# Reordering the retention stage of a hybrid trunk on Trainium2: projections of the first pair ahead of its keys, keys of the next pair ahead of the mixing of a pair

## The chip, the cores and the metric

The kernel runs on one core of one Trainium2 chip. The core has five engines that work side by side: TensorE (PE) for matmuls, VectorE (DVE) and ScalarE (ACT) for elementwise work on SBUF and PSUM, GpSimd (POOL) for elementwise work on SBUF, and SyncE (SP), which here only issues DMA transfers. Each engine takes its instructions in the order of its own queue. The metric is the time of one execution on the device, in microseconds, as the median of several runs.

## The reference, cut to what matters

A trunk of two layers works on 1024 latent tokens and 256 context tokens with 1024 channels. Each layer normalises and modulates its input, projects it once, gives the columns of that projection to three groups of heads (a pooling mixer, a 2-D neighbourhood attention, a bidirectional retention), joins their outputs, projects again, and runs a gated MLP. The retention is the part that matters here; it has six heads of 64 channels and goes over chunks of 128 tokens.

```python
def step(s, blk):
    qb, kb, vb = blk
    s_new = s * c_dec[None, :, None, None] + jnp.einsum('bhcd,bhce->bhde', kb * k_dec[None, :, :, None], vb)
    ...
    a = jnp.einsum('bhid,bhjd->bhij', qb, kb) * intra[None]
    y = jnp.einsum('bhij,bhje->bhie', a, vb) + jnp.einsum('bhid,bhde->bhie', qb, s) * q_dec[None, :, :, None]
    return s_new, y
...
def retention_output(y, gate, gn_g):
    ...
    mu = jnp.mean(y, axis=-1, keepdims=True)
    var = jnp.mean((y - mu) ** 2, axis=-1, keepdims=True)
    yn = ((y - mu) * lax.rsqrt(var + EPS)).reshape(B, L, RET_DIM) * gn_g.astype(jnp.float32)
    return (jax.nn.silu(gate.astype(jnp.float32)) * yn).astype(gate.dtype)
```

Both directions are computed and added. Query and key are rotated by a rotary embedding first (rows and columns of the token grid). The pooling mixer takes the difference between a moving mean over 2, 4, 8 or 16 tokens and the token itself, and multiplies it by a small matrix per group.

## The kernel before

Channels lie on the 128 partitions and tokens along the free axis. Tokens are cut into three parts: 512 and 512 latent tokens and 256 context tokens (`PARTS`). Every product of a projection is made of three matmuls of split operands (a high and a low half of the weights and of the input, lines 194 to 196), eight of these triples per part. The last layer needs no context output, so there queries and gates have two parts instead of three.

A projection is `feed` (line 329): it takes the next weights of a list, and for each part it takes one of two PSUM banks (tag `g`), runs 24 matmuls, and hands the bank to a body that drains it. The list is `plan` (lines 111 to 123): the weights are loaded, split and used strictly in that order, up to two ahead of their use, so it has to agree with the order of the calls. In the list, columns 9, 10, 11 of `w_in` are the queries of the three pairs of heads, 12 to 14 their keys, 15 to 17 their values, 18 to 20 their gates. Keys and values of the first two pairs, and the pooling mixer's input, are projected during the attention as its fillers and parked in DRAM (`r_dram`).

The stage is `ret()` (line 508), after the attention `nbr()` (line 337). Its pieces are:

- `tables()` (line 567): loads `dm` and makes the decay matrix `M` of each head with two Exp on ACT (lines 572 and 573) and three operations on POOL. Its scratch `e` has tag `qw`, `dm` has tag `ru`.
- `keys(p)` (line 590): for pairs 0 and 1 it loads key and value from `r_dram` into two tiles of tag `rw` (lines 595 and 596), for pair 2 it projects them (lines 601 and 605). It rotates the key (`rotary`, line 578, scratch `ru`), transposes values and keys on PE (lines 615 and 622, PSUM tag `t`), scales the keys by the decay into `kd` (lines 627 and 629), multiplies them with the values (line 634, `pk`, PSUM tags `sc` and `s`), and runs a scan over ten chunks on DVE that makes the states `S` (line 643).
- `query()` (line 646): projects the query, copies it from PSUM to `qw` (line 652) and rotates it into `qr`, which has one buffer. Its context part is copied straight to `qr` (line 582).
- `gate(p)` (line 658): projects the gate and applies Silu on ACT into `yn` (line 662, two buffers).
- `pool_mean(i)` and `pool_out(i)` (lines 526 and 554): the pooling mixer. It loads its input into `pb` (tag `rw`), makes moving sums on DVE in `sab`, which shares its one buffer with `kd`, multiplies on PE (line 559, `pps`, PSUM tag `o`), scales on ACT (line 560) and stores to `y_dram`.
- `mix(p, kr, vv, S, qr)` (line 665): in two or three blocks of up to four chunks, scores (line 677, `pa`, PSUM tag `s`), scores times `M` (line 679, `at`), query times state (line 684, `pf`, PSUM tag `sc`), scores times values (line 690, `py`, PSUM tag `o`), group normalisation on DVE, ACT and POOL (lines 692 to 703), a transpose back (line 706, `yps`, PSUM tag `t`) and the product with the gate (line 708).

PSUM tags `t` and `s` have two banks each, `sc` and `o` one each. The tile framework puts in all waits. It also orders the instructions of each engine when the program is built, by a timeline of its own: the order of the program text is a priority and the order in which buffers of one tag are handed out, but an instruction whose inputs are ready may be put ahead of earlier ones. `reuse_waits="tile"` lets a new pool start on addresses of an old one as soon as the single tiles there are done with.

After the stage, the outputs are loaded back from `y_dram` into `yna` (line 745), split, and the output projection `wo` starts (line 774); it adds into `h`, loaded at line 1541 or 1545, with the operation of line 782.

Of the kernel before, what the change touches and what calls it, by code (L numbers as in the profile page):

```python
# [45 lines left out]
def tile_trunk(ctx, tc, xT, ctxT, cc, ccT, w_mod, w_mod0, colp, w_in, pool_bd, rpbU, lgp, w_out, w_up, w_down, fing,  # L46
# [62 lines left out]
    fillers = (21, 22, 12, 15, 13, 16)  # L109
    plan, made, used, groups = [], [], [0], {}  # L110
    for l in range(DEPTH):
        for h in range(HEADS):
            plan += ([(w_in[l, h // 2], 0)] if h % 2 == 0 else []) + [(w_in[l, 3 + h], 4 if l == 0 and h == 1 else 1)]
            if h > 0:
                plan.append((w_in[l, fillers[h - 1]], 0))
        plan += [(w_in[l, i], 0) for i in fillers[5:] + (9, 18, 10, 19, 14, 17, 11, 20)]
        plan += [(w_out[l, o], 5 if o >= KT - 2 else 0) for o in range(KT)]
        names = UNITS if l == DEPTH - 1 else UNITS_C
        groups[l] = [(w_up[l, 2 * g], w_up[l, 2 * g + 1]) for g in range(NF)]
        groups[l] += [(w_down[l, 2 * g], w_down[l, 2 * g + 1]) for g in range(2 * NCH)]  # L120
        plan += [((l, g), (8, n)) for n in (FIRST if l == DEPTH - 1 else FIRST_C) for g in range(2)]
        plan += [((l, g), (8, n)) for g in range(2, NF + 2 * NCH) for n in names]
        plan += [(w_down[l, NF - 2], 3), (w_down[l, NF - 1], 0)]
# [84 lines left out]
    class Sums:  # L208
# [8 lines left out]
        def add(self, h, eng=None):  # L217
            if self.first:
                nc.scalar.activation(self.acc, h, AF.Square)
                self.first = False  # L220
                return
            sq = self.pool.tile([128, self.n], F32, tag="nt", name="sq", bufs=NT)
            nc.scalar.activation(sq, h, AF.Square)
            (eng or nc.gpsimd).tensor_tensor(self.acc, self.acc, sq, op=ALU.add)
# [96 lines left out]
    def mixing(l, X, mp):  # L321
# [7 lines left out]
        def feed(body, parts=(0, 1, 2), w=None):  # L329
            w = w or weights()  # L330
            for part in parts:
                o, n = PARTS[part]
                ps = psg.tile([128, 512], F32, tag="g", name="gps")
                gemm(ps, w, X, part)
                body(ps[:, :n], part, o, n)
# [172 lines left out]
        def ret():  # L508
# [17 lines left out]
            def pool_mean(i):  # L526
                pb = ra.tile([128, W], F32, tag="rw", name="pb", bufs=2)
                sab = ra.tile([128, 2, W], F32, tag="kd", name="sab", bufs=1)
                sa, sb = sab[:, 0], sab[:, 1]
                nc.gpsimd.memset(pb[:, 0:PADX], 0.0)  # L530
                nc.gpsimd.memset(pb[:, PADX + T:T + 3 * PADX], 0.0)
                nc.gpsimd.memset(pb[:, W - PADX:W] if not last else pb[:, T + 3 * PADX:W], 0.0)
                nc.sync.dma_start(pb[:, PADX:PADX + T], r_dram[i, :, 0:T])
                if not last:
                    nc.sync.dma_start(pb[:, T + 3 * PADX:W - PADX], r_dram[i, :, T:N])
                add = lambda o, a, b: nc.vector.tensor_tensor(o, a, b, op=ALU.add)
                if i == 0:
                    add(sa[:, 1:W], pb[:, 0:W - 1], pb[:, 1:W])
                    add(sb[high, 2:W - 1], sa[high, 1:W - 2], sa[high, 3:W])
                    srcs = ((low, sa), (high, sb))  # L540
                else:
                    add(sa[:, 1:W], pb[:, 0:W - 1], pb[:, 1:W])
                    add(sb[:, 2:W - 1], sa[:, 1:W - 2], sa[:, 3:W])
                    add(sa[:, 4:W - 3], sb[:, 2:W - 5], sb[:, 6:W - 1])
                    add(sb[high, 8:W - 7], sa[high, 4:W - 11], sa[high, 12:W - 3])
                    srcs = ((low, sa), (high, sb))
                for rows, S in srcs:
                    for (a, n) in ((PADX, T), (T + 3 * PADX, C))[:1 if last else 2]:
                        nc.vector.tensor_tensor(S[rows, a:a + 8], S[rows, a:a + 8], pcs[rows, i, 0:8], op=ALU.mult)
                        nc.vector.tensor_tensor(S[rows, a + n - 8:a + n], S[rows, a + n - 8:a + n], pcs[rows, i, 8:16], op=ALU.mult)  # L550
                        nc.vector.scalar_tensor_tensor(pb[rows, a:a + n], S[rows, a:a + n], pcs[rows, i, 16:17], pb[rows, a:a + n], op0=ALU.mult, op1=ALU.subtract)
                return pb

            def pool_out(i, pb):
                pbd = pbds[i]
                for part in yparts:
                    o, n = PARTS[part]
                    ps = psp.tile([128, 512], F32, tag="o", name="pps", bufs=1)
                    nc.tensor.matmul(ps[:, :n], pbd, pb[:, offs[part]:offs[part] + n], start=True, stop=True)
                    nc.scalar.mul(pb[:, offs[part]:offs[part] + n], ps[:, :n], cp[l][:, CP_PS + i:CP_PS + i + 1])  # L560
                nc.sync.dma_start(y_dram[3 + i, :, 0:T], pb[:, PADX:PADX + T])
                if not last:
                    nc.sync.dma_start(y_dram[3 + i, :, T:N], pb[:, T + 3 * PADX:W - PADX])
# [3 lines left out]
            def tables():  # L567
                dm = rp.tile([128, 512], F32, tag="ru", name="dm", bufs=2)
                nc.sync.dma_start(dm, dmat[:, 0:512])
                for h in range(HEADS):  # L570
                    e = ra.tile([128, 128], F32, tag="qw", name="e", bufs=2)
                    nc.scalar.activation(M[:, h], dm[:, 0:128], AF.Exp, scale=lg[:, h:h + 1])
                    nc.scalar.activation(e, dm[:, 256:384], AF.Exp, scale=lg[:, 6 + h:7 + h])
                    nc.gpsimd.tensor_tensor(M[:, h], M[:, h], dm[:, 128:256], op=ALU.mult)
                    nc.gpsimd.tensor_tensor(e, e, dm[:, 384:512], op=ALU.mult)
                    nc.gpsimd.tensor_tensor(M[:, h], M[:, h], e, op=ALU.add)

            def rotary(dst, t, part, eng=nc.gpsimd):
                o, n = PARTS[part]
                dst = dst[:, o:o + n]  # L580
                if part == 2:
                    nc.scalar.copy(dst, t)
                    return
                u = rp.tile([128, 512], F32, tag="ru", name="ru", bufs=2)
                nc.vector.stream_shuffle(u, t, [(j + 16) % 32 for j in range(32)])
                eng.tensor_tensor(dst, t, rope_sb[:, 0, o:o + n], op=ALU.mult)
                nc.vector.tensor_tensor(u, u, rope_sb[:, 1, o:o + n], op=ALU.mult)
                eng.tensor_tensor(dst, dst, u, op=ALU.add)
# [57 lines left out]
            def query():  # L646
                qr = rp.tile([128, N], F32, tag="qr", name="qr", bufs=1)

                def body(ps, part, o, n):
                    if part < 2:  # L650
                        t = ra.tile([128, 512], F32, tag="qw", name="qw", bufs=2)
                        nc.scalar.copy(t, ps)
                        ps = t
                    rotary(qr, ps, part)
                feed(body, yparts)
                return qr

            def gate(p):
                yn[p] = yp.tile([128, N], F32, tag="yn", name="yn", bufs=2)

                def body(ps, part, o, n):
                    nc.scalar.activation(yn[p][:, o:o + n], ps, AF.Silu)
                feed(body, yparts)
# [49 lines left out]
                    yt[5 + p] = yn[p]  # L713

            yn = {}
            for p in range(3):
                if p == 0:
                    tables()
                kk = keys(p)
                q = query()  # L720
                gate(p)
                if p == 0:
                    for i in range(2):
                        pool_out(i, pool_mean(i))
                mix(p, *kk, q)
            st.close()

        nbr()
        ret()
        return yt, psp  # L730

# [929 lines left out]
```

## Time and profile before

| what | value |
| --- | --- |
| median of three runs | 3078.0 us (3070.67 to 3079.22) |
| the profiled execution's own time | 3069.13 us |
| its span | 3067.3 us |
| mean granted TensorE clock over the span | 0.955 |
| DVE, ACT and POOL busy | 70%, 41% and 45% of the span |
| DVE's wait for the `rope` table ends | at 457.3 us in layer 0, 2059.9 us in layer 1 |

Times inside the profile count from the start of the span. The retention stage of layer 0 begins in the last blocks of the attention near 436 us and its last mix ends near 675 us; that of layer 1 goes from about 2042 us to 2243 us. A row of a timeline gives start, duration, engine, line, operation, output from inputs, shape and count, and in brackets the idle time ahead of it with what ended it. A row of busy time by stretch gives start and end, length, busy time with the count of instructions of each engine, the clock granted to TensorE as a share of full speed, the share of the DMA engines, and GB/s. SPq and ACTq are DMA issues of these engines; PEld are weight loads of TensorE, which run beside its matmuls.

### The profile page before, as it was taken

Reading aid. Unit: us, or ns where it says so; the run is one execution under the profiler, and the core shown is the slowest. Engines: PE = TensorE matmul, PEld = TensorE weight load, DVE = VectorE, ACT = ScalarE, POOL = GpSimd, SP = SyncE. Lnnn points to the kernel's source line nnn. Section 1 sums busy time; section 2 is a strip of 40 time slices with the busy share of each in tenths; the row PEclk is TensorE's granted clock in tenths of the full one; section 3 lists DMA queues with packets and bytes.
Section 4 is the critical chain, followed back from the end, with each engine's and each line's share of the span. In section 5 each row is a group of like instructions: output and inputs, shape, how many; then the busy total and the mean of one; then the engine's idle time right before and its main releaser. Section 6 shows DMA issues by size and latency. Waiting matters only on the chain. (4 is left out here: it accounts for less than half of the span.)

```text
span 3067.3 us, 40108 instructions
## 1 busy us (share of the span) xinstructions
PE 2791.9 (91%) x14430; PEld 2338.8 (76%) x14430; DVE 2146.8 (70%) x3468; ACT 1250.0 (41%) x2404; POOL 1366.0 (45%) x894
## 2 busy tenths in 40 slices
PE   6789989989989999998999799989997999998996
PEld 4678877878778787886888688877776788886775
DVE  7887745562878787788887755446547877778996
ACT  4345542232444443444333454542223544444332
POOL 4334343323335544554555244444242555554553
PEclk8899999989999999999999899999999999999998
DMA  6333321132133434346344112121252233335441
GB/s 217 85 113 114 95 97 66 37 138 71 51 111 128 135 126 143 126 139 204 117 128 118 50 50 61 45 102 59 76 195 87 83 103 104 103 110 206 137 138 62
DMA packets 166298, 332.02 MB, mean 108 GB/s; under 512 B 49490, under 2 KB 62674, under 8 KB 165842
## 3 DMA queue, kind: packets, MB, share of 16 engines
q1 hardware_dynamic: 165812, 328.28, 32.6%
q8 instruction: 114, 1.87, 0.3%
q10 hardware_dynamic: 288, 1.18, 0.1%
q14 instruction: 84, 0.69, 0.1%
HBM read 255.20 MB, written 74.19 MB: 107 GB/s over the span
## 5 line engine op out<-in xcount | busy, mean ns | idle before, releaser
L939 PE MATMUL ua<-ph,wu 128*128 128x512 f32 x1408 | 446.0, 398 | 14.3 <-DVE ub L1039 5.3
L165 POOL TENSOR_TENSOR wu<-urb,wu 128x512 fp32r<-128x512 f32 x160 | 250.5, 1566 | 330.7 <-ACT wu L164 325.4
L194 PE MATMUL gps<-xh,wh 128*128 128x512 f32 (+1 forms) x968 | 360.9, 373 | 17.6 <-ACT vt L269 7.0
L939 PE MATMUL ubc<-ph,wu 128*128 128x512 f32 x1056 | 335.3, 399 | 39.8 <-ACT ut L1033 28.6
L165 POOL TENSOR_TENSOR wu<-ura,wu 128x512 fp32r<-128x512 f32 x192 | 306.1, 1595 | 137.4 <-ACT wu L164 137.3
L195 PE MATMUL gps<-xh,wl 128*128 128x512 f32 (+1 forms) x968 | 356.3, 368 | 0.5 <-DVE wl L181 0.5
L196 PE MATMUL gps<-xl,wh 128*128 128x512 f32 (+1 forms) x968 | 355.7, 368 | 0.0
L426 POOL TENSOR_SCALAR P<-P,rs 128x640 f32<-128x640 f32 (+2 forms) x108 | 215.7, 2010 | 247.8 <-DVE rs L421 172.7
L939 PEld LDWEIGHTS ua<-ph,wu 128*128 128x128 f32 x1408 | 262.6, 191 | 74.1 <-ACT wu L164 6.4
L165 POOL TENSOR_TENSOR wu<-S,wu 128x512 fp32r<-128x512 f32 x128 | 181.6, 1421 | 259.9 <-ACT wu L164 257.3
L939 PE MATMUL ua<-pl,wu 128*128 128x512 f32 x704 | 279.2, 397 | 0.2 <-DVE pl L835 0.2
L939 PEld LDWEIGHTS ubc<-ph,wu 128*128 128x128 f32 x1056 | 199.3, 191 | 88.3 <-ACT ut L1033 33.4
L164 ACT CAST wu<-S 128x512 fp32r<-128x512 f32 x128 | 79.5, 621 | 402.5 <-DVE S L162 356.4
L186 POOL TENSOR_TENSOR wl<-wraw,wh 128x1024 fp32r<-128x1024 f32 x54 | 134.9, 2501 | 202.7 <-ACT wh L185 189.1
L194 PEld LDWEIGHTS gps<-xh,wh 128*128 128x128 f32 x968 | 185.5, 192 | 48.3 <-ACT vt L269 7.3
L939 PE MATMUL da<-ph,wu 128*128 128x512 f32 x640 | 203.8, 400 | 13.6 <-ACT wu L164 12.8
L939 PE MATMUL ubc<-pl,wu 128*128 128x512 f32 x528 | 208.5, 395 | 0.0
L195 PEld LDWEIGHTS gps<-xh,wl 128*128 128x128 f32 x968 | 185.6, 192 | 27.2 <-issue 1.5
L196 PEld LDWEIGHTS gps<-xl,wh 128*128 128x128 f32 x968 | 185.5, 192 | 26.3 <-issue 0.5
L164 ACT CAST wu<-ura 128x512 fp32r<-128x512 f32 x192 | 119.0, 622 | 131.5 <-DVE ura L162 61.5
L939 PE MATMUL dbc<-ph,wu 128*128 128x512 f32 x480 | 150.9, 396 | 10.1 <-DVE c L1099 10.1
L939 PEld LDWEIGHTS ua<-pl,wu 128*128 128x128 f32 x704 | 133.8, 190 | 31.7 <-DVE pl L835 1.5
(296 smaller groups left out, 6844.3 us busy)
## 6 DMA issues: line engine op xcount, KB each, us to landing
gs<-g_dram SPq DMA_DIRECT2D x148, 256.0 KB, 2.7
wm<-in_w_mod_dram SPq DMA_DIRECT2D x64, 512.0 KB, 3.9
wmp<-in_w_mod_dram SPq DMA_DIRECT2D x96, 256.0 KB, 2.7
wraw<-in_w_in_dram SPq DMA_DIRECT2D x46, 512.0 KB, 3.6
ura<-in_w_up_dram SPq DMA_DIRECT2D x44, 512.0 KB, 4.0
urb<-in_w_up_dram SPq DMA_DIRECT2D x44, 512.0 KB, 5.1
g_dram<-gt SPq DMA_DIRECT2D x60, 256.0 KB, 2.9
g_dram<-c SPq DMA_DIRECT2D x44, 256.0 KB, 2.1
```

The source lines that it names most:

```text
L164: nc.scalar.copy(w[:, 0], b[name])
L165: nc.gpsimd.tensor_tensor(w[:, 1], b[name], w[:, 0].bitcast(F32), op=ALU.subtract)
L186: nc.gpsimd.tensor_tensor(wl.rearrange(flat), raw.rearrange(flat), wh.rearrange(flat).bitcast(F32), op=ALU.subtract)
L194: nc.tensor.matmul(ps[:, :n], wh[:, k], xh, start=k == 0, stop=False)
L195: nc.tensor.matmul(ps[:, :n], wl[:, k], xh, start=False, stop=False)
L196: nc.tensor.matmul(ps[:, :n], wh[:, k], xl, start=False, stop=k == KT - 1)
L426: nc.gpsimd.tensor_scalar(Pb[r][:, :w], Pb[r][:, :w], rs[:, r:r + 1], None, op0=ALU.mult)
L939: nc.tensor.matmul(ps, lt, rt, start=start and j == 0 and q == 0, stop=j == len(x) - 1 and q == 2, skip_group_check=True)
```

## The change

The loop over the three pairs is written out in another order. Query and gate of pair 0 come first, ahead of `tables()` and `keys(0)`. `keys(1)` comes after the pooling mixer and ahead of `mix(0)`. After `mix(0)` the second query is projected, then `keys(2)` with its two projections, then the second gate, and only then `mix(1)`. The third query and gate stand between `mix(1)` and `mix(2)`. The list of weights follows: columns 14 and 17 (key and value of pair 2) now stand ahead of 19 (gate of pair 1). No piece is changed inside.

```diff
-        plan += [(w_in[l, i], 0) for i in fillers[5:] + (9, 18, 10, 19, 14, 17, 11, 20)]
+        plan += [(w_in[l, i], 0) for i in fillers[5:] + (9, 18, 10, 14, 17, 19, 11, 20)]
...
             yn = {}
-            for p in range(3):
-                if p == 0:
-                    tables()
-                kk = keys(p)
-                q = query()
-                gate(p)
-                if p == 0:
-                    for i in range(2):
-                        pool_out(i, pool_mean(i))
-                mix(p, *kk, q)
+            q = query()
+            gate(0)
+            tables()
+            kk = [keys(0)]
+            for i in range(2):
+                pool_out(i, pool_mean(i))
+            kk.append(keys(1))
+            mix(0, *kk[0], q)
+            q = query()
+            kk.append(keys(2))
+            gate(1)
+            mix(1, *kk[1], q)
+            q = query()
+            gate(2)
+            mix(2, *kk[2], q)
             st.close()
```

## The prediction

> **What bounds the kernel now.** I read the page first: TensorE carries the kernel.
>
> ```profile
> PE 2791.9 (91%) x14430; PEld 2338.8 (76%) x14430; DVE 2146.8 (70%) x3468; ACT 1250.0 (41%) x2404; POOL 1366.0 (45%) x894
> ```
>
> So a change is worth what it takes from TensorE's idle time and from its time at a low clock. The change touches only the retention stage, which runs once per layer, so the next view was busy time by stretch, for layer 0 and then layer 1. The columns are stretch, length, busy time and count for PE, PEld, DVE, ACT and POOL, granted clock, DMA share and GB/s.
>
> ```profile
> 436.50:453.00 16.50, 11.82 (x76) 9.13 (x74) 9.64 (x22) 9.00 (x26) 7.14 (x5) 1.00 0.08 14
> 453.00:469.20 16.20, 9.34 (x94) 7.25 (x94) 8.38 (x25) 8.44 (x23) 9.61 (x25) 0.58 0.58 199
> 469.20:506.00 36.80, 31.86 (x162) 26.34 (x160) 30.18 (x52) 7.90 (x13) 13.76 (x6) 0.91 0.12 43
> 506.00:622.00 116.00, 116.00 (x735) 97.79 (x735) 54.11 (x116) 27.58 (x52) 41.47 (x26) 1.00 0.14 47
> 622.00:634.50 12.50, 8.60 (x111) 6.64 (x109) 8.20 (x27) 6.96 (x14) 4.14 (x3) 1.00 0.50 177
> 634.50:652.00 17.50, 17.50 (x75) 15.53 (x76) 13.46 (x27) 10.66 (x24) 0.00 (x0) 0.53 0.42 168
> 652.00:669.00 17.00, 17.00 (x96) 13.41 (x94) 9.78 (x21) 2.77 (x6) 1.65 (x1) 0.99 0.00 0
> 669.00:678.20 9.20, 2.58 (x9) 1.30 (x8) 6.90 (x17) 2.60 (x7) 2.64 (x2) 0.71 0.71 240
> ...
> 2042.00:2054.00 12.00, 10.65 (x67) 8.72 (x67) 5.76 (x11) 6.94 (x17) 6.09 (x3) 1.00 0.16 53
> 2054.00:2072.00 18.00, 10.45 (x98) 7.87 (x97) 9.95 (x29) 9.53 (x26) 10.42 (x25) 0.63 0.48 164
> 2072.00:2090.00 18.00, 14.89 (x69) 11.37 (x68) 17.81 (x29) 3.89 (x5) 9.24 (x5) 0.97 0.03 5
> 2090.00:2102.00 12.00, 12.00 (x50) 8.64 (x52) 7.42 (x11) 1.69 (x3) 0.00 (x0) 0.74 0.37 136
> 2102.00:2190.00 88.00, 88.00 (x562) 74.03 (x559) 38.51 (x78) 21.80 (x40) 33.95 (x20) 1.00 0.14 44
> 2190.00:2211.00 21.00, 15.39 (x131) 11.76 (x130) 17.92 (x41) 6.62 (x13) 10.11 (x7) 0.92 0.34 116
> 2211.00:2240.00 29.00, 28.02 (x148) 23.88 (x148) 21.14 (x39) 10.78 (x21) 1.89 (x2) 0.82 0.37 137
> 2240.00:2250.00 10.00, 4.96 (x14) 3.85 (x15) 3.45 (x5) 1.77 (x3) 2.66 (x2) 0.66 0.74 258
> ```
>
> Three things are to be seen. The middle (506 to 622, and 2102 to 2190) is full at clock 1.00: nothing can be gained there. The entry (436.5 to 506) has 4.7 + 6.9 + 4.9 = 16.5 us idle in layer 0, and 1.35 + 7.55 + 3.1 = 12.0 us (2042 to 2102) in layer 1. The end (622 to 678.2) has 3.9 + 6.6 us idle, and 17.5 us at clock 0.53, which is 17.5 x 0.47 = 8.2 us lost. In layer 1 the end has 5.6 + 1.0 + 5.0 us idle and about 28 x 0.18 = 5 us lost to the clock. Over both layers idle time is 27.0 + 23.6 us and busy time times (1 - clock) about 16 + 15 us. So 82 us is the most that any order of this stage could save.
>
> **Why TensorE idles.** Next I read the timeline of each engine around those places.
>
> ```profile
> 436.42 0.39 PE L196 MATMUL gps<-xl,wh 128*128 128x512 f32 x1
> ...
> 468.31 1.07 ACT L652 COPY qw<-gps 128x512 f32<-128x512 f32 x2 [0.61 <-POOL M L576]
> ...
> 520.37 0.70 PE L559 MATMUL pps<-pb,pbd 128*128 128x256 f32 x2
> 526.08 1.00 PE L690 MATMUL py<-vv,at 128*128 128x64 f32 x8
> ...
> 526.90 0.69 DVE L679 TENSOR_TENSOR at<-pa,M 128x512 f32<-128x512 f32 x1 [10.43 <-PE py L690]
> ...
> 578.37 0.37 ACT L605 COPY vw<-gps 128x256 f32<-128x256 f32 x1 [2.97 <-PE gps L196]
> ...
> 621.52 0.61 PE L706 MATMUL yps<-ident,tm 128*128 128x128 f32 x4
> 621.97 0.38 PE L615 MATMUL vps<-ident,vw 128*128 128x128 f32 x2
> ```
>
> These rows show one rule: buffers of one tag are handed out in the order of the program text. The copies of the first query (`qw`) wait until 468 for `tables()` to give up `e`, which shares tag `qw`, though the second of their PSUM banks was filled with the matmul at 436.42; with both banks of tag `g` held, no projection can run, and the next one starts at 469.23 (shown below). `mix(0)`'s `py` comes only after the last `pps`, both on the single bank `o`. `keys(2)`'s transposes wait until 621.97 for the last `yps` of `mix(1)`, both on tag `t`, though `vw` was complete at 578.7. So keys and mixes alternate in a strict chain, and once the projections run out, the chain is bare.
>
> **The change, part by part.**
>
> *First query and gate ahead of tables and keys.* Nothing is added but order. I price one projection from its first and last matmul:
>
> ```profile
> 469.23 0.38 PE L194 MATMUL gps<-xh,wh 128*128 128x256 f32 x1
> ...
> 472.07 0.28 PE L196 MATMUL gps<-xl,wh 128*128 128x256 f32 x1
> 472.19 0.40 PE L194 MATMUL gps<-xh,wh 128*128 128x512 f32 x1
> ...
> 477.43 0.39 PE L196 MATMUL gps<-xl,wh 128*128 128x512 f32 x1
> ```
>
> A 512-column part is 24 matmuls in 5.5 us, a 256-column part 3.0 us, so a projection is 13.9 us in layer 0 and 10.9 us in layer 1. With `qw` first in its tag, each copy runs when its part is complete, the second at about 437; the banks come free, and the query's third part and the gate (3.0 + 13.9 = 16.9 us) can lie in the 11.5 us idle before 469. The rotation itself still waits for the rope table, whose load is issued late:
>
> ```profile
> 451.28 0.38 SPq L520 DMA_DIRECT2D rope_sb<-in_rope_dram  x1
> ```
>
> If the place of `qr` is no sooner free, the third part holds one bank until then and the gate runs on the other. Behind them come the second query and the first part of the keys' third projection, which fills a bank and then waits, since `kw` needs a slot of tag `rw` that the pool mixer gives up only through its store and reload:
>
> ```profile
> 508.49 0.32 SPq L595 DMA_DIRECT2D kw<-r_dram  x1
> ...
> 523.35 0.32 SPq L596 DMA_DIRECT2D vw<-r_dram  x1
> ```
>
> Up to 506 the old order did 16.9 us of these projections and one and a half parts more (8.2); the new one may do 16.9 + 13.9 + 5.5. That is 11.2 us ahead, less about 3 us of `mix(0)` that now waits for `keys(1)`: I take 8 us. The bounds are 0 (the idle time only moves behind 469) and 16.5 (all of it goes). In layer 1 the same count gives 7, between 0 and 12.0.
>
> What it costs: `keys(0)` gets its `ru` buffers after the query and `dm`, so I put it 3 to 5 us later; DVE's pool means (busy 30.18 of 36.8 us) then end near 501 rather than 498. It delays no TensorE work that is ready, so I count nothing; uncovered it is those 3 to 5 us per layer. The DMA of `dm` moves behind the first `ru` on SP's queue, past loads that wait for nothing later.
>
> *Silu ahead of Exp.* The first gate now runs between the attention's Exp and the tables' Exp, so ScalarE changes tables twice more per layer:
>
> ```profile
> 473.74 1.28 ACT L662 ACT_TABLE_LOAD   x1
> ```
>
> That is 4 x 1.28 = 5.1 us on an engine busy 8.4 of 16.2 us there; I count zero, up to 5 us if it lands in the attention's last chain. [...]
>
> *keys(1) ahead of mix(0), keys(2) ahead of mix(1).* Work is the same; the chain loses its bare keys. `keys(1)` now runs where `mix(0)` was blocked anyway (before 526), and `keys(2)` runs while gate and query of the third pair still fill TensorE. At the end the rows to go are these, and what is then late is the load of `h`:
>
> ```profile
> 632.12 2.38 DVE L643 SCALAR_TENSOR_TENSOR S<-S,cdec,pk 128x64 f32<-128x64 f32 x10 [0.62 <-PE pk L634]
> ...
> 634.46 1.20 PE L677 MATMUL pa<-qr,kr 64*128 64x128 f32 x8 [2.37 <-DVE S L643]
> ...
> 678.22 0.79 PE L194 MATMUL ops<-xh,wh 128*128 128x512 f32 x1 [2.31 <-DVE h L782]
> ```
>
> The wait for `h` (6.6 us idle) stays, since its buffers lie where the last mix works. Of the other 3.9 + 8.2 = 12.1 us in layer 0 I take half, 6, and give back 2 for new stalls of the in-order engines: 4 us, between -12 and +12. In layer 1, of 6.6 + 5 I take 4 and give back 3: 1 us, within the same bounds. [...]
>
> *The order of two weight loads* (14 and 17 ahead of 19) follows the calls; its cost is nothing, since the same bytes go in the same buffers. If it were not matched, projections would multiply the wrong weights, which is no matter of time.
>
> **The sum.** Layer 0: 8 + 4; layer 1: 7 + 1; together 20 us. The profiled execution took 3069.1 us (span 3067.3), so 3049 on its scale. It lies 9 us under the median of the runs shown, 3078.0, and I forecast on the median: 3058.
>
> **The rivals.**
>
> *The idle time only moves.* Both `g` banks can be stuck: in layer 0 the second query's third part goes straight to `qr`, which has one buffer and is held until `mix(0)` ends, and the other bank waits for `kw`. For it: between 486 and 506 TensorE would have little but pool outputs. Against it: 8 us of the entry's work really is earlier. Advance and new gap cancel: 3075.
>
> *Slower: mix(0) queued behind keys(1).* By the rule of tags, `pa` and `pf` (banks `s`, `sc`) now wait for `keys(1)`'s `pk`, hence for the reload of `vw`. If the pool outputs crawl as now, `vw` lands at about 526 (issue 523.35), and `keys(1)`, which before took
>
> ```profile
> 555.91 0.38 PE L615 MATMUL vps<-ident,vw 128*128 128x128 f32 x2
> ...
> 580.87 1.42 DVE L643 SCALAR_TENSOR_TENSOR S<-S,cdec,pk 128x64 f32<-128x64 f32 x7
> ```
>
> 26 us, ends at 552. Then come `mix(0)` with 35 (30 from its first `py` at 526.08 to 555.91, and my estimate of 5 for the `pa` and `pf` that were done before), `keys(2)` with 20 (between the 12.5 of its bare stretch and these 26), `mix(1)` with 39 (582.3 to 621.5) and `mix(2)` with 38 (634.46 to the row below): the mixes end at 684, against 673 now.
>
> ```profile
> 672.93 1.12 PE L706 MATMUL yps<-ident,tm 128*128 128x128 f32 x4 [3.15 <-DVE tm L703]
> ```
>
> That is +11 in layer 0; layer 1, whose pool outputs have two parts instead of three and whose reload thus comes sooner, I leave at zero: 3089. It decides from the point where `keys(1)`'s scan in layer 0 ends later than about 540. Against it: `pps` crawls now because `pa` stood ahead of it in TensorE's queue (4.9 us idle up to 506), and `pa` is now gone from there; I expect the scan to end near 526.
>
> *More than forecast.* With the scan at 526 the same count ends the mixes at 526 + 35 + 20 + 39 + 38 = 658, 15 us earlier, and the low clock at the end may go too (8.2 us). Some 20 us in each layer give 3038. Against it: the middle is full at clock 1.00 now, so the chain can shorten only as far as TensorE's own work is done earlier, and that advance was counted at 8 and 7 us.
>
> **How the numbers follow.** Forecast 0.50, idle time moves 0.20, slower 0.13, more 0.17. About 0.3% (9 us) is what a measurement of this kernel can tell from no change, so faster means under 3069. The forecast case lies there nine times in ten: faster 0.45 + 0.17 = 0.62, same 0.20 + 0.05 = 0.25, slower 0.13. The range reaches from a little beyond the strong case to the cancelled one and its spread, 3030 to 3082; it leaves out the slower case and the far ends, under 0.2.
>
> **What would show it.** Right, step by step: the first `qw` copy before 440 instead of 468; TensorE busy over 0.9 from 437 to 469; `keys(1)`'s scan before 540 and ahead of `mix(0)`'s first `py`; `vps` of `keys(2)` ahead of `mix(1)`'s `pa`; no wait for `S` ahead of `mix(2)`; two more table loads per layer. Wrong: a gap of over 10 us between 475 and 530 with both `g` banks full, mixes that end after 673, or a low clock that stays over the end of the stage although `keys(2)` is gone from it.

## The result and the profile after

The changed kernel takes 3104.3 us (median of 4 runs, 3097.64 to 3109.88), the kernel before 3074.3 us beside it (3070.63 to 3079.22). The ratio is 1.0097, with a 95% interval of 1.0081 to 1.0112: about 30 us **slower**, where 3058 us had been forecast with a range of 3030 to 3082.

First the line of busy time from the page of the changed kernel. TensorE has the same number of instructions; ScalarE has six more than the 2404 of before.

```profile
PE 2800.5 (90%) x14430; PEld 2347.6 (76%) x14430; DVE 2153.1 (70%) x3468; ACT 1257.8 (41%) x2410; POOL 1359.9 (44%) x894
```

Next, busy time by stretch of the changed kernel, layer 0 and then layer 1, with the columns of the prediction's table.

```profile
436.50:453.00 16.50, 15.55 (x102) 13.59 (x102) 8.09 (x19) 10.28 (x25) 10.71 (x7) 1.00 0.07 18
453.00:469.20 16.20, 15.73 (x94) 13.70 (x93) 4.49 (x13) 5.65 (x13) 2.43 (x2) 1.00 0.39 128
469.20:500.00 30.80, 26.09 (x177) 21.65 (x175) 23.67 (x44) 10.24 (x23) 17.27 (x29) 0.83 0.26 74
500.00:520.00 20.00, 8.49 (x18) 3.31 (x18) 15.46 (x29) 4.00 (x7) 5.99 (x4) 0.67 0.40 145
...
640.00:657.00 17.00, 16.80 (x76) 15.24 (x77) 12.70 (x21) 8.91 (x21) 3.43 (x3) 0.50 0.60 233
...
2090.00:2110.00 20.00, 11.47 (x102) 9.34 (x103) 16.78 (x34) 6.69 (x18) 12.15 (x23) 0.64 0.16 50
2110.00:2130.00 20.00, 12.78 (x38) 6.86 (x36) 15.94 (x25) 3.04 (x5) 3.02 (x3) 0.79 0.21 78
...
2230.00:2250.00 20.00, 19.11 (x81) 17.03 (x82) 16.73 (x27) 8.30 (x16) 4.46 (x3) 0.50 0.43 158
```

Up to 469 the forecast holds: 436.5 to 469.2 has 1.4 us idle where before had 11.5. Then the bill comes. From 500 to 520 TensorE works 8.5 of 20 us, in layer 1 from 2090 to 2130 24.3 of 40 us, and the end of the stage still has 17 and 20 us at a clock of 0.50.

To add this up, I count a stage from the issue of line 467 (`r_dram<-vt`) to the first `wo` matmul behind the wait for `h`, in slices of some 3 us; idle is the length of a slice less PE's busy time, "clock" is busy time times (1 - granted clock), and work is the rest. The clock column is an estimate of mine of what the low clock costs; in the changed kernel 32 matmuls of line 677 take 8.3 us between 636 and 660, at a granted 0.50, and 64 take 8.5 us between 536 and 620, at 1.00.

| stage | length | idle | clock | work |
| --- | --- | --- | --- | --- |
| before, layer 0 | 257.4 | 27.0 | 16.3 | 214.1 |
| after, layer 0 | 264.1 | 32.7 | 20.2 | 211.2 |
| before, layer 1 | 214.2 | 23.6 | 13.9 | 176.6 |
| after, layer 1 | 233.2 | 38.5 | 20.5 | 174.2 |

The two stages are 25.7 us longer, of the 28.5 us between the spans (3095.8 and 3067.3). The work did not grow. Idle time grew by 20.6 us and the loss to the clock by 10.5, mostly in **layer 1**.

The timeline of the changed kernel shows the steps:

```profile
442.31 1.09 ACT L652 COPY qw<-gps 128x512 f32<-128x512 f32 x2
462.18 0.28 PE L444 MATMUL po<-pw,V 128*128 128x256 f32 x1
504.43 0.28 DVE L643 SCALAR_TENSOR_TENSOR S<-S,cdec,pk 128x64 f32<-128x64 f32 x1
538.54 1.42 DVE L643 SCALAR_TENSOR_TENSOR S<-S,cdec,pk 128x64 f32<-128x64 f32 x7
640.20 2.07 PE L677 MATMUL pa<-qr,kr 64*128 64x128 f32 x8 [5.44 <-POOL qr L588]
683.35 0.69 PE L706 MATMUL yps<-ident,tm 128*128 128x128 f32 x2 [4.58 <-DVE tm L703]
686.17 0.79 PE L194 MATMUL ops<-xh,wh 128*128 128x512 f32 x1 [2.13 <-DVE h L787]
...
2039.71 0.33 SPq L467 DMA_DIRECT2D r_dram<-vt  x1
2080.43 0.28 PE L444 MATMUL po<-pw,V 128*128 128x256 f32 x1
2080.74 0.39 SPq L520 DMA_DIRECT2D rope_sb<-in_rope_dram  x1
2093.69 0.90 PE L634 MATMUL pk<-vv,kd 128*64 128x64 f32 x10 [4.53 <-DVE kd L629]
2097.98 1.09 PE L622 MATMUL kps<-ident,kr 128*128 128x128 f32 x4 [3.39 <-DVE kr L588]
2116.08 0.27 DVE L643 SCALAR_TENSOR_TENSOR S<-S,cdec,pk 128x64 f32<-128x64 f32 x1
```

The same places in the kernel before:

```profile
450.97 0.28 PE L444 MATMUL po<-pw,V 128*128 128x256 f32 x1
488.73 0.27 DVE L643 SCALAR_TENSOR_TENSOR S<-S,cdec,pk 128x64 f32<-128x64 f32 x1
675.22 0.69 PE L706 MATMUL yps<-ident,tm 128*128 128x128 f32 x2 [1.18 <-DVE tm L703]
...
2031.52 0.33 SPq L467 DMA_DIRECT2D r_dram<-vt  x1
2053.76 0.28 PE L444 MATMUL po<-pw,V 128*128 128x256 f32 x1
2054.07 0.38 SPq L520 DMA_DIRECT2D rope_sb<-in_rope_dram  x1
2089.49 0.27 DVE L643 SCALAR_TENSOR_TENSOR S<-S,cdec,pk 128x64 f32<-128x64 f32 x1
2158.76 2.38 DVE L643 SCALAR_TENSOR_TENSOR S<-S,cdec,pk 128x64 f32<-128x64 f32 x10 [5.45 <-PE pk L634]
```

The query's copies do run at 442 instead of 468. But its projections stand among the attention's last matmuls in PE's queue: the last `po` (the product that ends the attention) comes 40.7 us behind the start of layer 1's stage (2039.71 to 2080.43), before 22.2 us. The load of the rope table goes out right behind it, and `keys(0)` follows with PE waiting for DVE at each step; its scan ends at 504.7 us in layer 0, before at 489.0, and in layer 1 76.6 us behind the start of the stage, before 58.2. At the end of layer 0, PE waits 5.4 us for the last query's rotation.

### The profile page after: what moved, and what is told of

Same layout as the page of the kernel before. It is cut to its first block, busy times and chain, and to the rows that moved or that the text cites. A ratio compares the mean times of both kernels' runs of the same rounds, so it can differ in the third digit from the quotient of the medians.

```text
span 3095.8 us, 40121 instructions
## 1 busy us (share of the span) xinstructions
PE 2800.5 (90%) x14430; PEld 2347.6 (76%) x14430; DVE 2153.1 (70%) x3468; ACT 1257.8 (41%) x2410; POOL 1359.9 (44%) x894
## 5 line engine op out<-in xcount | busy, mean ns | idle before, releaser
L165 POOL TENSOR_TENSOR wu<-urb,wu 128x512 fp32r<-128x512 f32 x160 | 249.9, 1562 | 336.3 <-ACT wu L164 336.3
L164 ACT CAST wu<-ura 128x512 fp32r<-128x512 f32 x192 | 119.0, 622 | 131.6 <-DVE ura L162 61.2
```

Source lines behind the costliest of these rows:

```text
L164: nc.scalar.copy(w[:, 0], b[name])
L165: nc.gpsimd.tensor_tensor(w[:, 1], b[name], w[:, 0].bitcast(F32), op=ALU.subtract)
```

## The experiments

Three letters name the parts. **A**: query and gate of pair 0 ahead of the tables and of `keys(0)`. **B**: `keys(1)` ahead of `mix(0)`. **C**: `keys(2)` ahead of `gate(1)` and `mix(1)`, with the list of weights. Each diff is against the kernel before with its loop written out, or against the kernel named. Each run was timed against the kernel before in the same session (medians 3072.5 to 3075.4).

### Each part alone

```diff
 a_only
+            q = query()
+            gate(0)
             tables()
             kk = [keys(0)]
-            q = query()
-            gate(0)
 b_only
+            kk.append(keys(1))
             mix(0, *kk[0], q)
-            kk.append(keys(1))
 c_only
             q = query()
+            kk.append(keys(2))
             gate(1)
             mix(1, *kk[1], q)
-            kk.append(keys(2))
```

`bc_only` has both B and C. Expected of a_only:

> Query and gate of the first pair ahead of its tables and keys; the rest in the old order (mix(0) before keys(1), keys(2) after mix(1), old list of weights). Theory 1 (the projections in front stretch the end of the attention, so that the rope table and all that hangs on it come 10 to 18 us later in each layer): slower than before by 18 to 30 us, with the rope table's load issued near 462 us instead of 451 in layer 0. Theory 2 (the cause is keys(1) ahead of mix(0), which waits for the reload of kw and vw): within 6 us of before, or faster.

Of b_only:

> Only keys(1) ahead of mix(0); all else in the old order and with the old list of weights. Theory 1: within 6 us of before. Theory 2: slower by 15 to 30 us, most of it a wait of TensorE near 505 to 515 us for the reload.

Of bc_only:

> The first pair's tables, keys, query and gate in the old order; keys(1) ahead of mix(0) and keys(2) ahead of mix(1) as in the change. Theory 1: within 8 us of before, or faster. Theory 2: slower than before by 20 to 30 us.

Of c_only:

> Only keys(2) ahead of mix(1), with the new list of weights; the first pair and keys(1) in the old order. Theory 1 and theory 2 both expect no loss here: between 12 us faster and 3 us slower, since keys(2) leaves the bare end of the stage. If it is slower by over 6 us, a third cause lies in the end of the stage (the last query's rotation then follows mix(1) with nothing between).

| kernel | median, us | ratio to before | 95% interval |
| --- | --- | --- | --- |
| a_only | 3089.4 | 1.0050 | 1.0031 to 1.0068 |
| b_only | 3064.8 | 0.9968 | 0.9958 to 0.9977 |
| c_only | 3073.4 | 1.0000 | 0.9991 to 1.0010 |
| bc_only | 3084.1 | 1.0035 | 1.0022 to 1.0049 |

B alone **gains** some 10 us, so `mix(0)` behind the reload (theory 2) is not the cause. In layer 0 of b_only the scan of `keys(1)` ends at 536.3, before at 582.3:

```profile
534.86 1.42 DVE L643 SCALAR_TENSOR_TENSOR S<-S,cdec,pk 128x64 f32<-128x64 f32 x7
```

C costs nothing on the old order, but 19 us on top of B, and A about 14 us alone and 20 on top of B and C (3104.3 less 3084.1). So there are two losses to explain.

### Loss one: C on top of B

In bc_only the wait for the rotation is there again, and the end of layer 1 runs on at half clock. One row of its timeline, then four of its busy time by stretch:

```profile
631.70 2.07 PE L677 MATMUL pa<-qr,kr 64*128 64x128 f32 x8 [5.44 <-POOL qr L588]
```

```profile
2195.00:2205.00 10.00, 10.00 (x43) 9.09 (x43) 3.49 (x8) 0.47 (x1) 0.08 (x1) 0.50 0.00 0
2205.00:2215.00 10.00, 4.81 (x20) 4.03 (x20) 8.13 (x17) 1.26 (x2) 4.60 (x4) 0.50 0.00 0
2215.00:2225.00 10.00, 8.77 (x45) 8.43 (x46) 6.99 (x9) 1.96 (x4) 4.47 (x3) 0.50 0.85 318
2225.00:2235.00 10.00, 10.00 (x35) 8.47 (x35) 9.84 (x18) 6.37 (x13) 0.00 (x0) 0.50 0.13 51
```

Counted as in the stage table, the two stages of bc_only are 18.5 us longer than those of b_only; about 16 us of this are lost to the clock and only 4 us are idle time.

`qr` has one buffer, which `mix(1)` holds. The first try splits it, so that each part is free as soon as the mixing has read it.

```diff
 bc_qrp, against bc_only
...
-                qr = rp.tile([128, N], F32, tag="qr", name="qr", bufs=1)
+                qr = [rp.tile([128, PARTS[part][1]], F32, tag=f"qr{part}", name=f"qr{part}", bufs=1) for part in yparts]
...
+                        qp = qr[b0 // 4]
...
-                            nc.tensor.matmul(pa[:, j], kr[rows, sl], qr[rows, sl], start=True, stop=True)
+                            nc.tensor.matmul(pa[:, j], kr[rows, sl], qp[rows, j * 128:(j + 1) * 128], start=True, stop=True)
...
```

> bc_only with the query's rotated rows in three tiles, one for each part of the tokens, in place of one: a part can be rotated as soon as the mixing has read that part, so that the rotation of the last query no longer waits for the whole of mix(1). Theory that C costs by the last query's rotation in the end (PE waits 5.4 us there for POOL in layer 0): 8 to 14 us less than bc_only, so back to b_only (about 3066 to 3072). Rival (C costs because the end of the stage is then made of mixing alone, in small matmuls at a granted clock of 0.50 for 40 to 50 us, whatever the rotation does): within 5 us of bc_only, 3078 to 3086.

Measured: 3086.1 us, ratio 1.0041 (1.0024 to 1.0058), no better. But its timeline shows why (line numbers are one or two higher here):

```profile
625.42 2.79 DVE L705 TENSOR_TENSOR tm<-tm,va 128x512 f32<-128x512 f32 x1
630.09 0.72 DVE L586 STREAM_SHUFFLE ru<-qw 128x512 f32<-128x512 f32 x1
630.71 0.67 DVE L702 TENSOR_REDUCE va<-d 128x8 f32<-128x512 f32 x1
631.97 0.73 DVE L586 STREAM_SHUFFLE ru<-qw 128x512 f32<-128x512 f32 x1
```

The rotation's scratch `ru` and the mixing's squares `d2` share one tag with two buffers, handed out in program order. So the second of the last query's two shuffles (631.97) cannot run until `mix(1)`'s last squares have been reduced (630.71), whatever `qr` does. The second edit takes them apart:

```diff
 bc_qrd2, against bc_qrp; the same two edits make b_qrd2 of b_only
-                    d2 = rp.tile([128, 8, 64], F32, tag="ru", name="d2", bufs=2)
+                    d2 = rp.tile([128, 8, 64], F32, tag="d2", name="d2", bufs=2)
 bc_d2, against bc_only: this edit alone
```

> bc_qrp with one more edit: the squares of the mixing (d2) get two buffers of their own instead of sharing the two of the rotation's product (ru). In the trace of bc_qrp the last query's rotation did not wait for qr any more but for ru: its shuffle on VectorE starts at 630.1 us, behind the squares of mix(1), and PE still waits 4.1 us for it. Theory that C costs by this rotation in the end: the waits of mix(2)'s first pa for POOL (4.1 us in layer 0, 4.3 in layer 1) go, the ends of mix(1) on VectorE (yps waits of 9.4 and 6.9 us) shrink, and the time falls by 8 to 16 us to 3068 to 3077. Rival (the end made of mixing alone, at a granted clock of 0.50, is the cost whatever the rotation does): the waits go, but the time stays within 5 us of bc_only and bc_qrp, 3080 to 3090.

> b_only with the same two edits as bc_qrd2 (three tiles for the query's rotated rows, own buffers for the squares). If rotation and mixing hold each other up by these buffers in any order, it falls by 4 to 10 us below b_only, to 3055 to 3061, and is the fastest kernel so far; if they only do where C makes mixing the end, it stays within 3 us of b_only's 3065.

> bc_only with the second edit alone: own buffers for the squares, the query's rotated rows still in one tile. Theory that the two together hold the last query's rotation back (one buffer by qr, the other by ru): 3072 to 3086, most of the 23 us between bc_only and bc_qrd2 still missing. Rival (ru alone did it): 3058 to 3066, as bc_qrd2.

| kernel | median, us | ratio to before | 95% interval |
| --- | --- | --- | --- |
| bc_qrd2 | 3061.2 | 0.9946 | 0.9928 to 0.9964 |
| b_qrd2 | 3068.0 | 0.9974 | 0.9965 to 0.9984 |
| bc_d2 | 3068.3 | 0.9989 | 0.9979 to 0.9999 |

With both edits 23 us are gone by the medians and the order B + C is faster than before; without C the same edits bring nothing (b_only 0.9968, b_qrd2 0.9974). The squares' buffers alone bring 16 of the 23. In bc_qrd2 the rotation ends on POOL at 626.9 and `mix(2)`'s first `pa` runs without a wait:

```profile
625.64 1.27 POOL L589 TENSOR_TENSOR qr<-qr,ru 128x512 f32<-128x512 f32 x1
628.64 0.37 PE L679 MATMUL pa<-qr,kr 64*128 64x128 f32 x1
```

In bc_d2 it still waits, for the one `qr`:

```profile
629.15 1.71 PE L677 MATMUL pa<-qr,kr 64*128 64x128 f32 x8 [3.10 <-POOL qr L588]
```

So loss one is shown for the order B + C: C puts a rotation beside a mixing with which it shares its buffers, and with the buffers apart the loss is gone. By the count of the stage table, bc_qrd2 has about 13 us less idle time than bc_only and 10 us less lost to the clock, the latter in layer 0 alone, where bc_only goes to half clock in the stretch of the wait (first row) and bc_qrd2 does not (second row):

```profile
624.00:631.00 7.00, 1.11 (x4) 0.71 (x4) 6.79 (x14) 0.63 (x1) 4.06 (x4) 0.51 0.22 75
624.00:631.00 7.00, 6.95 (x61) 6.21 (x61) 6.21 (x14) 1.58 (x3) 2.83 (x2) 1.00 0.77 259
```

In layer 1 the clock costs 24 us in both by that count. One thing stays open: c_only has the same wait, in layer 1 alone, where its stage is 221.2 us long instead of 214.2, and yet its time is that of the kernel before.

```profile
2207.22 2.07 PE L677 MATMUL pa<-qr,kr 64*128 64x128 f32 x8 [7.53 <-POOL qr L588]
```

### Loss two: A

**Is it the uncovered moving sums?** Both before_nosum (old order) and a_nosum (order of a_only) leave out the moving sums of the pooling mixer, so that its output is only the scaled difference of the raw rows:

```diff
-                add = lambda o, a, b: nc.vector.tensor_tensor(o, a, b, op=ALU.add)
...
-                        nc.vector.scalar_tensor_tensor(pb[rows, a:a + n], S[rows, a:a + n], pcs[rows, i, 16:17], pb[rows, a:a + n], op0=ALU.mult, op1=ALU.subtract)
+                        nc.vector.scalar_tensor_tensor(pb[rows, a:a + n], pb[rows, a:a + n], pcs[rows, i, 16:17], pb[rows, a:a + n], op0=ALU.mult, op1=ALU.subtract)
```

> The old order, with the moving sums of the pool mixer left out (its output is then only the scaled difference of the raw rows): L536, L549 and L550 of VectorE, 8.8 + 3.7 + 3.4 + 1.2 = 17.1 us per layer in the trace of before, are gone, and with them the longest part of the chain from keys(0) to the pool outputs. Cover theory (in before the query and gate projections of pair 0 cover that chain, about 30 us of it in 436-500): a gain of 3 to 8 us, not 34. Rival (the chain of VectorE sets the end in before too): a gain of 20 to 34 us. It is the partner of a_nosum.

> The order of a_only, with the same moving sums left out as in before_nosum. Cover theory (a_only lost because its projections stretch the attention's end and are used up when VectorE works through the 17 us of moving sums bare): the distance to before_nosum shrinks from the 14 us of a_only to 0 to 6 us. Rival (the loss is the stretched end of the attention itself, 10 us in layer 0 and 18 in layer 1, or the table loads, whatever comes behind): the distance stays 11 to 20 us.

Measured: 3063.3 us (0.9961, 0.9946 to 0.9975) and 3079.4 (1.0017, 1.0003 to 1.0032). Both orders gain about 10 us and the distance stays, 16 us: it is not the sums.

**Is it the rope table?** In b_rb the pool of the constants is opened first, so that the rope table falls on other memory.

```diff
 b_rb, against b_only
-            ra, rb, rp = [st.enter_context(tc.tile_pool(name=f"{n}{l}", bufs=1, reuse_waits="tile")) for n in ("ra", "rb", "rp")]
+            rb, ra, rp = [st.enter_context(tc.tile_pool(name=f"{n}{l}", bufs=1, reuse_waits="tile")) for n in ("rb", "ra", "rp")]
```

> b_only with one line changed: the pool of the constants (rope table, pcs, pbd) is opened ahead of the pool of the working buffers, so that the rope table falls on memory that the attention gives back at another time. Theory that the entry of the stage hangs on the rope table, whose load is issued only behind the attention's last copy (451.3 us in before): if the load goes out earlier, the entry's idle time (11.2 us in layer 0, 10.2 in layer 1 of b_only) falls by 3 to 5 us per layer and the time by 5 to 12 us against b_only. Rival (keys(0)'s own rows, or VectorE, are ready no earlier, or the working buffers take over the late place): within 4 us of b_only.

Measured: 3065.7 us (0.9977, 0.9963 to 0.9991), as b_only. The load goes out at 395.7 us, ahead of the attention's end, and the scan of `keys(0)` ends 63.0 instead of 67.8 us behind the start of layer 0's stage, but nothing comes of it: without A the rope table is not the limit.

**Is it the stretched end of the attention?**

```diff
 a_tab, against a_only
-            q = query()
-            gate(0)
             tables()
+            q = query()
+            gate(0)
             kk = [keys(0)]
```

> a_only with two steps changed about: the tables first, then the first pair's query and gate, then keys(0). The query's copies share their two buffers with the six tables, so the projections can no longer go into the attention's last steps, but they are still ahead of keys(0) and of the pool mixer in the order. Theory (A costs because its projections are put among the attention's last matmuls, where only 4.7 and 1.4 us are idle, stretch its end from 30 to 40 us and from 22 to 41 us, and are then missing as cover behind it): the last po matmul is back at 30 and 22 us behind the stage's start, and the time is that of before, 3070 to 3079. Rival (what costs is that keys(0) and the pool mixer stand behind the projections in the order): still 10 to 18 us slower than before, 3085 to 3093.

Measured: 3093.2 us (1.0058, 1.0040 to 1.0076). The last `po` is back at 30.1 and 22.2 us, but the loss stays: this theory falls too. Three rows of a_tab's timeline in layer 1 show where the time went instead:

```profile
2067.16 0.86 DVE L643 SCALAR_TENSOR_TENSOR S<-S,cdec,pk 128x64 f32<-128x64 f32 x4 [0.99 <-PE pk L634]
2094.36 1.42 DVE L643 SCALAR_TENSOR_TENSOR S<-S,cdec,pk 128x64 f32<-128x64 f32 x5 [3.88 <-PE pk L634]
2215.61 1.12 PE L706 MATMUL yps<-ident,tm 128*128 128x128 f32 x4 [9.67 <-DVE tm L703]
```

The projections now lie between the first and the second block of `keys(0)`: its scan stands still for 26 us (2068.0 to 2094.4). Later PE waits 9.7 us in one piece for `mix(1)`.

a_tab also answers for the table loads of ScalarE. With the tables ahead of the gate it has not one more than the kernel before, as its page shows (2404 ScalarE instructions, where a_only has 2408), and it loses as much as a_only:

```profile
PE 2793.7 (91%) x14430; PEld 2341.0 (76%) x14430; DVE 2147.1 (70%) x3468; ACT 1250.1 (41%) x2404; POOL 1354.2 (44%) x894
```

**Is it the shared buffers again?** The two edits of bc_qrd2 on a_only, on the kernel before and on the whole change:

> a_only with the same two buffer edits. In a_only and a_tab PE waits 9.6 us in one piece in layer 1 for the last step of mix(1) on VectorE (2.2 us in before), which there stands among the rotations of keys(2) and of the last query. Theory of the shared scratch buffers: that wait falls to 2 to 4 us, and the time to 3072 to 3080, within 5 us of before_qrd2. Rival (A costs because the work that hides the chain of keys, pool mixer and mixing is spent ahead of it, whatever the buffers): the waits move, and it stays 10 to 18 us slower than before_qrd2, 3084 to 3093.

> The kernel before with the same two buffer edits: the partner of a_qrd2. In the old order the mixing of a pair is followed by the next pair's keys and query, whose rotations also take their product's buffers behind the squares; but b_qrd2 stayed at b_only's time, so it stays within 5 us of before, 3069 to 3079. If it falls by 6 us or more, the buffers hold the old order up as well.

> The whole change with the two buffer edits of bc_qrd2 (three tiles for the query's rotated rows, own buffers for the squares of the mixing). Theory that the change loses by rotation and mixing handing each other two scratch buffers, in all its steps: 24 to 40 us less than the changed kernel, 3062 to 3080. Rival (step A, the first pair's projections ahead of its keys, loses by itself; bc_qrd2 plus the 14 to 18 us of a_only and a_tab): 3073 to 3082, between 12 and 20 us above bc_qrd2. To tell them apart a_qrd2 counts, and the distance to bc_qrd2's 3061.

Measured: a_qrd2 3077.3 us (1.0022, 1.0009 to 1.0035), before_qrd2 3067.6 (0.9983, 0.9971 to 0.9995), after_qrd2 3085.7 (1.0041, 1.0025 to 1.0056). A still costs 10 us on the old order and 24 us on B + C.

**Which half?** The query alone ahead (bcq_qrd2), the gate alone ahead (bcg_qrd2, with columns 18 and 9 changed about in the list of weights):

```diff
 bcq_qrd2, against bc_qrd2
+            q = query()
             tables()
             kk = [keys(0)]
-            q = query()
             gate(0)
 bcg_qrd2, against bc_qrd2
+            gate(0)
             tables()
             kk = [keys(0)]
             q = query()
-            gate(0)
```

> bc_qrd2 with one half of step A: the first pair's query ahead of the tables and of keys(0), its gate where it was. after_qrd2, with both halves, is 24 us above bc_qrd2. Theory of VectorE's order (the query's rotation then stands ahead of the rotation of keys(0) behind the load of the rope table, and everything behind keys(0) is later by it): nearly the whole loss, 14 to 24 us above bc_qrd2, 3075 to 3085. Theory of the spent cover (what counts is how much projection work is left behind keys(0), and the query is half of it): 6 to 13 us above, 3067 to 3074.

> bc_qrd2 with the other half of step A: the first pair's gate ahead of the tables and of keys(0), its query where it was. It has no rotation and only its copies on ScalarE. Theory of VectorE's order: within 4 us of bc_qrd2, 3057 to 3066. Theory of the spent cover: 6 to 13 us above it, 3067 to 3074, as bcq_qrd2.

Measured: 3082.4 us (1.0040, 1.0023 to 1.0058) and 3080.8 (1.0030, 1.0017 to 1.0043). Each half costs about as much as both, which fits neither theory. The halves are not clean: with the query ahead, the gate's projections follow it into the attention (last `po` again at 40.7 us in layer 1). The gate ahead puts Silu between Exp operations of the attention, with table loads at 439.39, 441.79 and 444.60 us in layer 0; bcg_qrd2 has 2416 ScalarE instructions, after_qrd2 2410.

**And the other way?**

```diff
 bc_late_qrd2, against bc_qrd2
             kk = [keys(0)]
-            q = query()
-            gate(0)
             for i in range(2):
                 pool_out(i, pool_mean(i))
             kk.append(keys(1))
+            q = query()
+            gate(0)
             mix(0, *kk[0], q)
```

> The opposite of step A on bc_qrd2: the first pair's query and gate stand behind its keys, behind the pool mixer and behind keys(1), ahead of mix(0). Theory of the chain (A costs because it delays the head of a chain that runs from keys(0) through pool mixer, reload, keys(1) and keys(2) to the end of the stage: in layer 1 the scan of keys(0) ends 58 us behind the stage's start in every kernel without A and 69 to 77 in those with it, and keys(2)'s scan 157 against 169 to 178): keys(0)'s scan stays at 68 and 58 us, the last pool output comes 5 to 15 us earlier than the 90 and 72 of bc_qrd2, and the time is that of bc_qrd2 or lower, 3050 to 3064. Theory of the spent cover (projections must stand beside the chain of keys(0) and pool mixer to fill its waits, whichever way they are moved): 8 to 20 us above bc_qrd2, 3069 to 3081.

Measured: 3060.1 us (0.9958, 0.9944 to 0.9972), the time of bc_qrd2. The cover theory, which asked for 8 to 20 us more, falls. What the kernels have in common shows in the positions of four rows of layer 1, in us behind the start of its stage: the last `po` of the attention, the last `pps`, the end of the scan of `keys(1)`, and the first `wo` matmul.

| kernel | last `po` | last `pps` | scan of `keys(1)` ends | stage ends |
| --- | --- | --- | --- | --- |
| before | 22.2 | 73.3 | 129.6 | 214.2 |
| before_nosum | 22.2 | 61.3 | 119.7 | 216.5 |
| a_only | 40.7 | 92.3 | 146.6 | 236.6 |
| a_tab | 22.2 | 88.8 | 146.1 | 231.5 |
| bc_qrd2 | 22.2 | 72.1 | 98.9 | 218.9 |
| bc_late_qrd2 | 22.2 | 66.2 | 102.5 | 216.0 |
| bcg_qrd2 | 32.0 | 80.3 | 108.2 | 220.3 |
| bcq_qrd2 | 40.7 | 86.1 | 120.1 | 237.4 |
| after_qrd2 | 40.7 | 85.9 | 119.0 | 231.7 |

Wherever projections stand ahead of `keys(0)` or inside it, the last `pps` and the scan of `keys(1)` come later by 8 to 21 us, and most of that reaches the end, save in bcg_qrd2; where they stand behind it, nothing is lost. Each row is one execution. The scan of `keys(1)` repeats well from kernel to kernel (98.9 to 99.0 us in b_only, b_qrd2, bc_only, bc_qrp, bc_d2 and bc_qrd2); the last column is less sure, since the profiled execution of a_only took 10 us more than its median, those of bcq_qrd2 and bc_qrd2 8 and 6 us more. Earlier than in the kernel before, the chain brings this layer nothing (before_nosum: scan 10 us earlier, stage no shorter). That TensorE's own work is the limit there, as the full middle of the stage suggests, is argued and not shown. Layer 0 has three parts to project instead of two, and takes up part of the delay (after_qrd2 249.9 us, bc_qrd2 244.5); bcg_qrd2 loses there (261.0), not in layer 1. By the count of the stage table, after_qrd2 has about 21 us more idle time than bc_qrd2 and no more lost to the clock: unlike loss one, this is a loss of waits.

So it is shown that A loses by itself, without the sums, without the stretched attention, without the table loads and without the shared buffers, each taken away by itself, and that the opposite move does not lose. That the late chain `keys(0)` - pool mixer - reload - `keys(1)` carries the loss fits all of these rows, but a kernel that delays `keys(0)` with the projections left in place was not tried.

bc_qrd2 and bc_late_qrd2, at 0.9946 and 0.9958, are the fastest orders found, about 0.5% ahead of the kernel before.

## Why the prediction was wrong, point by point

- **Where PE idles and why**: right. The rule that buffers of one tag are handed out in program order is what the rows showed again, with `ru`.
- **First query and gate: 8 + 7 us gained**: the step that failed. The mechanism came (`qw` at 442, 436.5 to 469.2 filled), the gain did not. The prediction took the 11.5 us idle ahead of 469 for free room. A projection put there stands in PE's one queue among the attention's dependent matmuls (76 matmuls of projections between 436.5 and 462.3, two between 436.5 and 451.1 in the kernel before), and the last of these dependent ones came 11.2 us later in layer 0 (462.18 instead of 450.97) and 18.5 us in layer 1, counted from the start of the stage. `keys(0)`, put 3 to 5 us later, ended its scan 15.7 us later in layer 0 (504.7 instead of 489.0) and 18.4 us in layer 1, and 20 us of it stood at the scan of `keys(1)` in layer 1 (after_qrd2 against bc_qrd2). So "It delays no TensorE work that is ready, so I count nothing" was the wrong price: the delay reached the end, by the chain behind it as far as the rows show. In place of +15 us stood -14 (a_only) to -20 us (on B and C).
- **Silu ahead of Exp**: counted as nothing, and no run speaks against that. The six more ScalarE instructions of the page are table loads of 1.28 us each, nine instead of three in and around the two stages, where four more had been counted; ScalarE is 7.8 us longer busy. a_tab loses as much as a_only without a load more, so they are not loss two. In the changed kernel a load at 597.99 has work on both sides: the activation ahead of it ends at 597.97, and the next one starts at 599.28, 0.01 us behind the load.
- **keys(1) ahead of mix(0)**: right, and alone worth 10 us. In the changed kernel its scan ends at 540.0, just where the prediction put the point of decision, 14 us later than it expected.
- **keys(2) ahead of mix(1): 4 + 1 us gained, half of the low clock gone**: wrong on top of B, where it cost 19 us (bc_only against b_only). The 2 us given back for new stalls missed that `ru` and `qr` tie the last rotation to the mixing. With buffers apart the sign was right: bc_qrd2 is 7 us faster than b_qrd2 by the medians, and their intervals just miss each other.
- **The wait for h stays**: right, 2.13 us against 2.31.
- **The slower rival** gave 3089, with the mixes of layer 0 ending at 684; their last transposes begin at 683.35 and end at 684.0. That is luck: its mechanism, `mix(0)` behind the reload, was not the cause (b_only gains), its scan of `keys(1)` was to end at 552 and ended at 540, and it left layer 1 at zero, where most of the loss was. Its 673 for the kernel before is also not the end but the block ahead of it; the last transposes there begin at 675.22.

## What to carry to other kernels

Work that can run at any time is the filler of a dependent chain: put it behind the chain's head in the program. Ahead of the head it filled 10 idle microseconds of layer 0 here, and cost 10 to 24 us in all; behind it, it cost nothing. Before two pieces are moved beside each other, list every scratch tag that they share; here a tag of two small tiles made a good step cost 16 us and more. And time each part of a reorder alone and in pairs: this one was a gain of 10 us and two losses of some 20.

## What the runs showed of the hardware

**Half clock through busy stretches.** In the four stretches of bc_only above, PE counts as busy for 33.6 of 40 us and is granted 0.50 all the while; by the count of the stage table that is 16.8 us lost. In layer 1 of bc_qrd2 it is granted 0.50 through 37 us in which it counts as busy without a break:

```profile
2174.00:2190.00 16.00, 16.00 (x77) 15.09 (x77) 6.90 (x11) 1.58 (x3) 5.40 (x4) 0.50 0.16 43
2190.00:2211.00 21.00, 21.00 (x80) 18.60 (x81) 17.79 (x34) 8.21 (x16) 3.65 (x2) 0.50 0.43 168
```

**VectorE beside GpSimd.** In bc_qrp the step `tm<-tm,va` at 625.42 took 2.79 us, beside the first row below; with GpSimd idle, as beside the second, it took 0.69 us.

```profile
625.32 2.34 POOL L186 TENSOR_TENSOR wl<-wraw,wh 128x1024 fp32r<-128x1024 f32 x1
...
664.43 0.69 DVE L705 TENSOR_TENSOR tm<-tm,va 128x512 f32<-128x512 f32 x1 [1.82 <-POOL va L704]
```

The slow step ended 0.55 us after GpSimd's row (628.21 and 627.66). In the changed kernel the same step took 1.89 us at 631.70, beside a row of GpSimd that ran from 630.70 to 633.04, and again ended 0.55 us after it; at 563.82 it took 0.63 us, though a row of GpSimd had begun at 563.79. What decides this was not shown.
